# Moved operands of the dense products in the upper half of SBUF, their weights in the lower half

## The chip, the core and the metric

The kernel runs as one program on one core of a Trainium2 chip. The metric is the time of one execution in device microseconds; the figure that counts is the median over several runs. One execution was profiled as well, and its rows are what the text below quotes. Lower is better.

## What is computed

A decoder trunk of two layers over 1024 tokens with a width of 1024, all in float32. Layer 0 has a forgetting attention with a pooling mixer, layer 1 an RWKV-7 time mix; each is followed by a gated feed-forward block of width 2816.

```
def _swiglu(h, w_gate, w_up, w_down):
    return (jax.nn.silu(h @ w_gate) * (h @ w_up)) @ w_down

def reference(x, ...):
    for layer in range(DEPTH):
        h = _rmsnorm(x, mix_norm[layer])
        if layer % 2 == 0:
            y = _fox_pool_mixer(h, hy_w_in[e], ...)      # h @ w_in, attention, pooling, @ w_out
        else:
            y, v_first = _rwkv7_time_mix(h, ...)          # xr @ w_r, xk @ w_k, xv @ w_v, scan, @ w_o
        x = x + y
        x = x + _swiglu(_rmsnorm(x, ffn_norm[layer]), ...)
    return x
```

## The kernel before

**Dense products.** Tokens lie along the free dimension in two halves of 512, features along the partitions. A dense product therefore multiplies a 128x128 block of weights, which TensorE holds still, with a 128x512 tile of inputs, which it moves through. Each float32 operand is split into a high and a low part in float32r, and `mm3` (line 155) forms a product as three matmuls: high by high (line 162), low moved part by high weights (line 163), high moved part by low weights (line 164):

```
nc.tensor.matmul(out, wh, xh, start=(first and i == 0), stop=False)
nc.tensor.matmul(out, wh, xl, start=False, stop=False)
nc.tensor.matmul(out, wl, xh, start=False, stop=(last and i == n - 1))
```

There are 3088 such triples of the full size that the change is about, 9264 matmuls. In the profile a row `mm<-uh,whi` reads: output `mm` (or `fm`), moved tile `uh`, weights `whi`; the letter h or l at the end says high or low part.

**Weights.** `load_part` (line 141) brings a 128x512 piece by DMA into `wraw`, casts it on ScalarE to `whi` and subtracts on VectorE for `wlo`. Weight tiles come from the pool `wf` from the start on, from the pool `w4` for the last stage, and a few small ones from `wl`. `pair` (line 249) makes the two parts of a moved tile, `part` (line 256) fills them.

**Stages.** (1) `fox` (line 313): the normed input H lies in the pool `h`; projections, attention and pooling run woven into each other. (2) Output projection, from the same pool `h`. (3) First feed-forward block, lines 1355 to 1367: half 0 moves tiles from the pool `u`; half 1 moves tiles from the pool `m1` (their name in the profile is `h1`), and most of half 1 is kept as filler `f1`. (4) `rw.dense(0, ...)`: projections of the time mix for half 0; the moved tiles again come from `u`. (5) The time mix of half 0 (`rw.job`), with `f1` woven in. (6) `tail(0, ...)` (line 1381), the output projection and second feed-forward block of half 0, moving tiles `h` and `g` from the pool `tail0`, woven into `rw.dense(1, ...)`, which moves `mx` tiles from the pool `mb`, and then into the time mix of half 1. (7) `tail(1, ...)` from the pool `tail1`, alone at the end.

**What sets the order and the addresses.** The instructions are put in order at build time from the order of the code and from when buffers come free. Pools are stacks: a pool of side left gets the next free bytes from the bottom of each partition, a pool of side right from the top down, and a closed pool gives its bytes back. The side and the order in which pools are opened thus set every address. A tile of a dense product, moved or weights, takes 2048 bytes of each partition, and the blocks of weights within it start every 512 bytes.

The lines that the change touches most are 323 (side of the pool `fox`), 353 and 1280 (which buffers a split goes to), 1267 to 1272 and 1303 to 1304 (opening of pools), 1332 to 1341, 1366, 1390, 1402, 1407, 1419 and 1450.

Of the kernel before, what the change touches and what calls it, by code (L numbers as in the profile page):

```python
# [197 lines left out]
def chain(*gens):  # L198
    for g in gens:
        yield from g  # L200
# [48 lines left out]
def pair(k, pool, tag, bufs, n=HN):  # L249

    hi = pool.tile([P, n], F32R, tag=tag, name=nm(k, tag + "h"), bufs=bufs)
    lo = pool.tile([P, n], F32R, tag=tag, name=nm(k, tag + "l"), bufs=bufs)
    return hi, lo


def part(k, hl, raw):
    hi, lo = hl
    k.nc.scalar.copy(hi, raw)  # L258
    k.nc.vector.tensor_tensor(lo, raw, rd(hi), ALU.subtract)  # L259
    return hi, lo  # L260


def use_ln_exp(k, after=None):

    i = k.nc.scalar.preload_act_table_set("natural_log_exp_and_others")
    if after is not None:
        k.tc.add_manual_dep(i.ins, after.ins.name, mybir.DependencyInfo(mybir.DependencyClass.NoSync, mybir.DependencyReason.DATA),
                            reason="act table")
# [44 lines left out]
def fox(k, ins, H, hpool, xpools, y, then, r_att):  # L313
# [6 lines left out]
    k.tmpbufs=5  # L320
    nc, tc = k.nc, k.tc
    ctx = ExitStack()
    ap_ = ctx.enter_context(tc.tile_pool(name="fox", bufs=1, side="right", reuse_waits="tile"))

    def tmp(n):
        return ap_.tile([P, HN + 16], F32, tag="tmp", name=nm(k, n), bufs=k.tmpbufs)
# [19 lines left out]
    def load_x(half, at={}):  # L346
        n = Norm(k, None, tmp)
        for kt in range(KT):
            if kt in at:
                at[kt]()  # L350
            t = xtile(k, xpools[half])[:, 1:]
            nc.sync.dma_start(t, ins["xT"][kt * P:(kt + 1) * P, half * HN:half * HN + HN])
            hi, lo = H[half][kt] = pair(k, hpool, "h", 32)
            nc.scalar.activation(hi, t, AF.Copy, scale=cvec(k, "mix0", kt))  # L354
            nc.vector.scalar_tensor_tensor(lo, t, cvec(k, "mix0", kt), rd(hi), ALU.mult, ALU.subtract)
            n.add(t)
            xs[half].append(t)
        return n
# [314 lines left out]
def make_h(k, norm, gain, x, acc, out, rs=None):  # L673
    nc = k.nc
    rs = rs or norm.rstd()
    for kt in range(KT):
        t = norm.tile("hn")
        nc.vector.scalar_tensor_tensor(t, x[kt], cvec(k, gain, kt), rs, ALU.mult, ALU.mult)
        out[kt] = part(k, pair(k, *acc), t)


def ffn(k, ins, L, halves, H, X, acc, tp, groups, after=None, silu=True, fb0=0):
    nc = k.nc

    def project(w):
        o = {half: pmm(k) for half in halves}
        for c in range(2):
            for half in halves:
                yield from mm3(k, o[half], [(blk(w, kt), H[half][kt]) for kt in range(4 * c, 4 * c + 4)], c == 0, c == 1)
        return o  # L690

    def down(n, fb0, acts, last):
        per = max(1, 4 // n)
        cur = None
        for half, m in [(half, m) for half in halves for m in range(8)] if last else [(half, m) for m in range(8) for half in halves]:
            if cur != m // per:
                cur = m // per
                w = []
                for f in range(0, n, 4):
                    c = min(4, n - f)  # L700
                    w.append(load_part(k, ins[f"wd{L}"][per * cur:per * cur + per, :, fb0 + f:fb0 + f + c].rearrange("m p f c -> p m f c"), P, per * c * P))
            o = pmm(k)
            yield from mm3(k, o, [(blk(w, (m % per) * n + i), acts[fb0 + i, half]) for i in range(n)])
            nc.vector.tensor_tensor(X[half][m], o, X[half][m], ALU.add)  # L704
            if last:
                after(half, m)


    behind = iter(())
    for gi, n in enumerate(groups):  # L710
        acts, sgs = {}, {}
        for fb in range(fb0, fb0 + n):
            g = yield from project(load_w(k, ins[f"wg{L}"][fb]))
            for half in halves:
                sg = sgs[half] = tp.tile([P, HN], F32, tag="nt", name=nm(k, "sg"), bufs=k.ntbufs)
                if silu:
                    k.last_silu = nc.scalar.activation(sg, g[half], AF.Silu)
                elif silu is None and k.sigm:
                    k.last_sig = nc.scalar.activation(sg, g[half], AF.Sigmoid)
                    nc.vector.tensor_tensor(sg, g[half], sg, ALU.mult)  # L720
                else:
                    nc.scalar.activation(sg, g[half], AF.Exp, scale=-1.0)
                    nc.scalar.activation(sg, sg, AF.Ln, bias=1.0)
                    nc.scalar.activation(sg, sg, AF.Exp, scale=-1.0)
                    nc.vector.tensor_tensor(sg, g[half], sg, ALU.mult)  # L725
            yield from behind
            behind = iter(())
            u = yield from project(load_w(k, ins[f"wu{L}"][fb]))
            for half in halves:
                sg = sgs[half]  # L730
                nc.vector.tensor_tensor(sg, u[half], sg, ALU.mult)
                acts[fb, half] = part(k, pair(k, *acc), sg)
        behind = down(n, fb0, acts, after and gi == len(groups) - 1)
        fb0 += n
    yield from behind
# [497 lines left out]
def build(ctx, tc, ins, outs, dbg=None, stop=99):  # L1233
    nc = tc.nc
    k = K()
# [11 lines left out]
    def pool(n, side="left"):  # L1247
        c = ExitStack()
        p = c.enter_context(tc.tile_pool(name=n, bufs=1, side=side, reuse_waits="tile"))
        return c, p  # L1250
# [13 lines left out]

    stream(k, 1)
    use_ln_exp(k)
    c_x0, x0 = pool("x0")
    c_wf, wf = pool("wf", "right")
    c_x1, x1 = pool("x1", "right")
    xp = (x0, x1)  # L1270
    c_h, hpool = pool("h")
    c_ps, k.ps = psum("ps0")
    k.mm, k.sbufs = (k.ps, "mm", 3), 2
    k.wp, k.wbufs, k.rawbufs, k.ntbufs = wf, 5, 2, 6
# [2 lines left out]
    LATE = 3  # L1277

    def split_y(kt, half):
        sp[kt, half] = part(k, pair(k, hpool, "h", 32), y[kt][half])  # L1280

    def out_tile(half, m):
        XT[half][m] = xtile(k, xp[half])
# [16 lines left out]
                nc.vector.tensor_tensor(x, o, x, ALU.add)  # L1300

    fox(k, ins, H, hpool, xp, y, oproj_early(), [3.2, 2.8, 2.8])
    c_m, mp = pool("m1", "right")
    c_t, tp = pool("t1", "right")
    wo = [load_part(k, ins["w_out"][4 * i:4 * i + 4, :, LATE * P:LATE * P + P].rearrange("m p c -> p m c"), P, 512) for i in range(2)]
    w7 = load_w(k, ins["w_out"][7])
    def out_block(half, m, last):
# [22 lines left out]
            on[1].add(x)  # L1330
    c_h.close()
    c_wl, wl = pool("wl")
    c_u, u = pool("u")
    U, M = (u, "u", 40), (mp, "h1", 24)
    make_h(k, on[0], "ffn0", X[0], U, H[0], rs0)
    c_ps.close()
# [1 line left out]
    c_ps, k.ps = psum("ps1")  # L1338
    k.mm = (k.ps, "mm", 4)

    norms = [Norm(k, tp), Norm(k, mp)]

    cover = [lambda: None, lambda: ahead(project, 0)]

# [18 lines left out]
    run(ffn(k, ins, 0, (0, 1), H, X, U, tp, G0, fb0=sum(GP)))  # L1363
    run(ffn(k, ins, 0, (0,), H, X, U, tp, G1, after0, True, n))
    rw.ln_exp, rw.mx, rw.wl_bufs, k.sigm = False, U, 2, True
    f1 = chain(ffn(k, ins, 0, (1,), H, X, M, mp, GP, silu=None), ffn(k, ins, 0, (1,), H, X, M, mp, G2, after0, None, n))
    f1 = using(k, f1, mm=(pf, "fm", 2), ntbufs=3)
    lead, share = (96, 0)
    ahead(f1, lead)
    weave(rw.dense(0, XT[0], wl, tp), (f1, share))  # L1370
    for c in (c_u, c_wl, c_x0, c_t, c_ps):
        c.close()
    c_ps, k.ps = psum("ps2")
    k.sbufs = 3
# [3 lines left out]
    use_ln_exp(k, k.last_sig)  # L1378
    k.mm, k.sigm, rw.ln_exp = (pf, "fm", 2), False, True

    def tail(half, p, ng, silu):

        norm = Norm(k, p)

        def project():
            sp = []
            for kt in range(KT):
                t = norm.tile("y")
                nc.sync.dma_start(t, rw.dt(f"y{kt}_{half}"))
                sp.append(part(k, pair(k, p, "h", 16), t))  # L1390
            yield 0
            for m in range(8):
                hl = load_w(k, ins["w_o"][m])
                o = pmm(k)
                yield from mm3(k, o, [(blk(hl, kt), sp[kt]) for kt in range(KT)])
                x = X[half][m] = p.tile([P, HN], F32, tag="x4", name=nm(k, "x"), bufs=8)
                nc.sync.dma_start(x, rw.dt(f"x{m}_{half}"))
                nc.vector.tensor_tensor(x, o, x, ALU.add)
                norm.add(x)

        def rest():
            make_h(k, norm, "ffn1", X[half], (p, "h", 16), H[half])

            def after1(half, m):
                nc.sync.dma_start(outT[m * P:(m + 1) * P, toks(half)], X[half][m])

            yield from ffn(k, ins, 1, (half,), H, X, (p, "g", 2 * ng), p, (4, 4, 4, 4, 4, 2), after1, silu)

        return project(), rest()

# [5 lines left out]
    c_ps, k.ps = psum("ps3")  # L1416
    k.mm, k.ntbufs = (k.ps, "mm", 4), 6
    c_t, tp = pool("tail0")
    project, rest = (using(k, g, mm=(pf, "fm", 2), ntbufs=3) for g in tail(0, tp, 4, False))
    Y1 = 1  # L1420
    if Y1:
        next(project)
    run(f1)
    c_m.close()
    c_mb, mb = pool("mb", "right")
    rw.mx, rw.wl_bufs, rw.ln_exp = (mb, "mx", 36), 2, "0"=="1"
    d1 = rw.dense(1, XT[1], mb, mb, ((2, "k", 1), (3, "v", 4), (0, "r", 5)))
# [19 lines left out]
    c_ps.close()  # L1447
    c_ps, k.ps = psum("ps5")
    c_w, wp4 = pool("w4")
    c_l, lp = pool("tail1")  # L1450
    project, rest = (using(k, g, mm=(k.ps, "mm", 3), wp=wp4, wbufs=7, ntbufs=3) for g in tail(1, lp, 8, True))
    weave(project, (fill, TS))
    run(fill)
    run(rest)
    for c in (c_l, c_w, c_t, c_wf, c_ps, c_pf):
        c.close()


# [89 lines left out]
```

## Time and profile before

| | before |
|---|---|
| median of 3 runs | 2720.83 us (2717.3 to 2724.43) |
| the profiled execution | 2725.7 us |
| its span, first to last instruction | 2723.9 us, mean granted clock 0.992 |
| busy time of TensorE's matmuls, 15368 records | 2665.5 us (98%) |
| busy time of its weight loads | 2080.5 us (76%) |
| busy time of VectorE, ScalarE | 1725.1 us (63%), 1297.9 us (48%) |

The profile counts a matmul as busy from its start to the modelled end of its last result, so neighbouring matmuls overlap, and a busy share of 98% says only that TensorE hardly rests. How fast it goes is read from the distance between the starts of two matmuls, or from how many of them fit into a stretch of time. The weight load of the next matmul runs beside the current one and has its own rows (PEld).

### The profile page before, as it was taken

How to read it: one execution, taken by the hardware profiler on the slowest of the kernel's cores; microseconds unless marked ns; L12 is line 12 of the kernel's file. 1: busy time of each engine (PE TensorE's matmuls, PEld its weight loads, DVE VectorE, ACT ScalarE, POOL GpSimd, SP SyncE). 2: the span in 40 equal slices, each digit the busy share in tenths (PEclk: the TensorE clock that was granted, in tenths of full speed). 3: DMA queues.
4: the chain of work that ended last, by engine and by line, in shares of the span. 5: the costliest groups of instructions: out<-in, count | busy, mean ns of one | idle time of the engine just before them, and what ended most of it. 6: DMA issues, size and time to landing. Idle time of an engine off the chain costs nothing.

```text
span 2723.9 us, 40262 instructions
## 1 busy us (share of the span) xinstructions
PE 2665.5 (98%) x15368; PEld 2080.5 (76%) x15368; DVE 1725.1 (63%) x2940; ACT 1297.9 (48%) x2297; POOL 50.0 (2%) x139
## 2 busy tenths in 40 slices
PE   9999999999999999999999999999999999999999
PEld 6777778778888777777777677777777777788887
DVE  7777684653336655975995676569769856544443
ACT  7555564442224766534644467655445344333232
POOL 1000000000001000000000000000000000000000
PEclk9999999999999999999999999999999999999999
DMA  4111131233333445423533534454344236333332
GB/s 134 57 51 57 41 96 51 82 93 94 94 96 112 159 164 179 132 88 95 175 93 98 185 105 154 163 184 128 90 136 136 86 98 201 104 97 97 97 97 93
DMA packets 170241, 306.11 MB, mean 112 GB/s; under 512 B 18608, under 2 KB 25904, under 8 KB 170048
## 3 DMA queue, kind: packets, MB, share of 16 engines
q1 hardware_dynamic: 156224, 278.38, 32.8%
q10 hardware_dynamic: 13824, 25.17, 2.5%
q8 instruction: 120, 1.97, 0.3%
q14 instruction: 73, 0.60, 0.1%
HBM read 257.04 MB, written 46.43 MB: 111 GB/s over the span
## 4 chain that ended last, share of the span: by engine, by line
PE 82%; DVE 11%; ACT 3%; DMA 2%; issue 2%; SPq 0%; ACTq 0%; DVEq 0%
PE mm L162 17%; PE mm L163 16%; PE mm L164 16%; PE fm L162 7%; PE fm L164 6%; PE fm L163 6%; DVE wlo L151 2%; PE mm L174 1%; DVE nu L1109 1%; DVE pd L1107 1%; PE s L1057 1%; PE o L1174 1%; PE s L1162 1%; PE s L1168 1%; PE o L1187 1%
## 5 line engine op out<-in xcount | busy, mean ns | idle before, releaser
L150 ACT CAST whi<-wraw 128x512 fp32r<-128x512 f32 x738 | 453.1, 616 | 891.6 <-PE mm L163 493.0
L151 DVE TENSOR_TENSOR wlo<-wraw,whi 128x512 fp32r<-128x512 f32 x738 | 500.9, 683 | 455.9 <-ACT whi L150 445.5
L162 PE MATMUL mm<-hh,whi 128*128 128x512 f32 x864 | 345.1, 401 | 5.8 <-ACT hh L354 5.7
L164 PE MATMUL mm<-hh,wlo 128*128 128x512 f32 x864 | 340.4, 394 | 0.0
L163 PE MATMUL mm<-hl,whi 128*128 128x512 f32 x864 | 339.5, 394 | 0.0
L164 PE MATMUL mm<-uh,wlo 128*128 128x512 f32 x728 | 287.3, 395 | 1.4 <-DVE wlo L151 1.4
L162 PE MATMUL mm<-uh,whi 128*128 128x512 f32 x728 | 287.7, 397 | 0.9 <-DVE x L1315 0.9
L163 PE MATMUL mm<-ul,whi 128*128 128x512 f32 x728 | 287.5, 396 | 0.0
L162 PE MATMUL fm<-h1h,whi 128*128 128x512 f32 x528 | 220.7, 418 | 14.0 <-DVE sg L725 9.9
L163 PE MATMUL fm<-h1l,whi 128*128 128x512 f32 x528 | 210.1, 398 | 0.1
L164 PE MATMUL fm<-h1h,wlo 128*128 128x512 f32 x528 | 209.7, 397 | 0.5 <-DVE wlo L151 0.5
L162 PEld LDWEIGHTS mm<-hh,whi 128*128 128x128 f32 x864 | 162.8, 189 | 42.6 <-ACT hh L354 6.5
L164 PEld LDWEIGHTS mm<-hh,wlo 128*128 128x128 f32 x864 | 162.8, 188 | 35.9 <-DVE wlo L151 0.6
L163 PEld LDWEIGHTS mm<-hl,whi 128*128 128x128 f32 x864 | 163.2, 189 | 33.6 <-DVE hl L259 1.5
L162 PE MATMUL fm<-hh,whi 128*128 128x512 f32 x416 | 174.5, 420 | 3.2 <-ACT hh L258 2.7
L164 PE MATMUL fm<-hh,wlo 128*128 128x512 f32 x416 | 167.9, 404 | 0.0
L163 PE MATMUL fm<-hl,whi 128*128 128x512 f32 x416 | 167.7, 403 | 0.2 <-DVE hl L259 0.2
L162 PEld LDWEIGHTS mm<-uh,whi 128*128 128x128 f32 x728 | 136.4, 188 | 38.7 <-issue 3.5
L163 PEld LDWEIGHTS mm<-ul,whi 128*128 128x128 f32 x728 | 136.6, 188 | 35.8 <-issue 1.1
L164 PEld LDWEIGHTS mm<-uh,wlo 128*128 128x128 f32 x728 | 136.5, 188 | 35.0 <-DVE wlo L151 2.2
L704 DVE TENSOR_TENSOR x<-mm,x 128x512 f32<-128x512 f32 x96 | 66.2, 692 | 122.8 <-PE mm L164 122.5
L162 PEld LDWEIGHTS fm<-h1h,whi 128*128 128x128 f32 x528 | 100.4, 190 | 48.1 <-DVE sg L725 12.3
(338 smaller groups left out, 4642.5 us busy)
## 6 DMA issues: line engine op xcount, KB each, us to landing
wraw<-in_wg_dram SPq DMA_DIRECT2D x176, 256.0 KB, 2.8
wraw<-in_wu_dram SPq DMA_DIRECT2D x176, 256.0 KB, 2.7
wraw<-in_wd_dram SPq DMA_DIRECT2D x176, 256.0 KB, 2.7
wraw<-in_w_in_dram SPq DMA_DIRECT2D x52, 256.0 KB, 2.9
x<-in_xT_dram SPq DMA_DIRECT2D x32, 256.0 KB, 4.6
x<-x SPq DMA_DIRECT2D x32, 256.0 KB, 3.6
wraw<-in_w_k_dram SPq DMA_DIRECT2D x32, 256.0 KB, 2.8
wraw<-in_w_v_dram SPq DMA_DIRECT2D x32, 256.0 KB, 3.0
```

Of the source, the lines that this page charges most:

```text
L150: k.nc.scalar.copy(hi[0:p, 0:n], raw[0:p, 0:n])
L151: k.nc.vector.tensor_tensor(lo[0:p, 0:n], raw[0:p, 0:n], rd(hi[0:p, 0:n]), ALU.subtract)
L162: nc.tensor.matmul(out, wh, xh, start=(first and i == 0), stop=False)
L163: nc.tensor.matmul(out, wh, xl, start=False, stop=False)
L164: nc.tensor.matmul(out, wl, xh, start=False, stop=(last and i == n - 1))
L174: k.nc.tensor.matmul(out[n * q:n * q + n], w[:, n * j:n * j + n], xs[j], start=c == 0, stop=c + g == len(xs), tile_position=(0, n * q))
L704: nc.vector.tensor_tensor(X[half][m], o, X[half][m], ALU.add)
L1057: nc.tensor.matmul(scs[h][:, 128 * c:128 * c + 128], bk[HS[h], 4 * b + c], ZL[h][HS[h], i, 4 * b + c], start=True, stop=True)
L1107: nc.vector.tensor_tensor(pv, nu[:, j + 1:32, j:j + 1].broadcast_to([P, n, j]), nu[:, j:j + 1, 0:j].broadcast_to([P, n, j]), ALU.mult)
L1109: nc.vector.tensor_tensor(nu[:, j + 1:32, 0:j], nu[:, j + 1:32, 0:j], pv, ALU.add)
L1162: nc.tensor.matmul(z[HS[h], i], ZL[h][:, i, c, 0:64], SV[h][:, i, c], start=True, stop=True)
L1168: nc.tensor.matmul(u[HS[h], i], XR[HS[h], i, c, 0:64], zs[HS[h], i], start=True, stop=True)
```

## The change

The pools of weights go to the left side, the pools of moved tiles to the right side. The pool `h` goes: H and the split attention outputs get the pool `m1` for twelve of sixteen pairs and a new pool `h2` for the other four. `m1` is opened at the start and stays open to the end; `tail(0, ...)` takes its pairs from it too, instead of from `tail0`, so that its inputs, its activations and those of the block before it share one ring of 24 buffers. A small new pool `n1` takes the norm's and the gate's work tiles of half 1. Operations, shapes and counts of instructions stay.

The core of the diff:

```
-    ap_ = ctx.enter_context(tc.tile_pool(name="fox", bufs=1, side="right", reuse_waits="tile"))
+    ap_ = ctx.enter_context(tc.tile_pool(name="fox", bufs=1, side="left", reuse_waits="tile"))
...
-            hi, lo = H[half][kt] = pair(k, hpool, "h", 32)
+            hi, lo = H[half][kt] = pair(k, *hpool[8 * half + kt >= 12])
...
+    c_wf, wf = pool("wf")
     c_x0, x0 = pool("x0")
-    c_wf, wf = pool("wf", "right")
+    c_m, mp = pool("m1", "right")
     c_x1, x1 = pool("x1", "right")
+    c_h, h2 = pool("h2", "right")
-    c_h, hpool = pool("h")
+    hpool = (mp, "h1", 24), (h2, "h2", 8)
...
-    c_m, mp = pool("m1", "right")
-    c_t, tp = pool("t1", "right")
+    c_t, tp = pool("t1")
...
-    c_u, u = pool("u")
+    c_n, np_ = pool("n1", "right")
+    c_u, u = pool("u", "right")
...
-    f1 = chain(ffn(k, ins, 0, (1,), H, X, M, mp, GP, silu=None), ...)
+    f1 = chain(ffn(k, ins, 0, (1,), H, X, M, np_, GP, silu=None), ...)
...
-                sp.append(part(k, pair(k, p, "h", 16), t))
+                sp.append(part(k, pair(k, *hs), t))
...
-    project, rest = (... for g in tail(0, tp, 4, False))
+    project, rest = (... for g in tail(0, tp, 4, False, M, M))
...
-    c_l, lp = pool("tail1")
+    c_l, lp = pool("tail1", "right")
```

Where the built programs put the pools (bytes from the start of a partition; the middle of the 224 KiB is 114688):

| pool, what for | first to last byte before | first to last byte after |
|---|---|---|
| `wf`, weights | 204768 to 229344 | 4608 to 29184 |
| `w4`, weights of the last stage | 76288 to 109056 | 51712 to 84480 |
| `wl`, small weights of the time mix | 21248 to 31488 | 64256 to 74496 |
| `h` (after: `m1` and `h2`), moved | 21248 to 86784 | 180192 to 229344 and 147168 to 163552 |
| `u`, moved | 31488 to 113408 | 75488 to 157408 |
| `m1`, moved | 132832 to 188128 | 180192 to 229344 |
| `mb`, moved | 85728 to 188128 | 61152 to 163552 |
| `tail0` (after: `m1`), moved | 4608 to 76288 | 180192 to 229344 |
| `tail1`, moved | 109056 to 197120 | 92128 to 180192 |
| `fox`, attention | 87488 to 188128 | 45824 to 146464 |
| `core`, `core2`, time mix | 4608 to 132736, 76288 to 204416 | 29184 to 157312, 51712 to 179840 |

Of the 9264 full-size matmuls, those that move a tile of `u` are 2184, of `h` 1344, of `tail0` 1776, of `m1` 1584, of `mb` 600, of `tail1` 1776; the weights are in `wf` for all but the last, which has `w4`.

The order of instructions changes in few places, all of them where a split waits for a buffer. On ScalarE, at the splits of the eight `y` tiles of `tail(0, ...)` (the cast at line 258, out `hh` from `y`; `whi` are casts of weights, `sg` gates of `f1`), before:

```order
L150 CAST whi_14433<-wraw_14435 128x512
L258 CAST hh_14258<-y_14256 128x512
L258 CAST hh_14264<-y_14262 128x512
L258 CAST hh_14270<-y_14268 128x512
L150 CAST whi_14439<-wraw_14441 128x512
L258 CAST hh_14276<-y_14274 128x512
L150 CAST whi_14475<-wraw_14477 128x512
L258 CAST hh_14282<-y_14280 128x512
L258 CAST hh_14288<-y_14286 128x512
```

The same place after the change, where the tiles are named `h1h` since they are cut from `m1`:

```order
L150 CAST whi_14583<-wraw_14585 128x512
L722 ACTIVATE sg_14473<-fm_14448 128x512
L258 CAST h1h_14285<-y_14283 128x512
L723 ACTIVATE sg_14473<-sg_14473 128x512
L258 CAST h1h_14291<-y_14289 128x512
L724 ACTIVATE sg_14473<-sg_14473 128x512
L258 CAST h1h_14297<-y_14295 128x512
L150 CAST whi_14615<-wraw_14617 128x512
L258 CAST h1h_14303<-y_14301 128x512
```

The first four splits stay near their place, the last four move behind four to five casts of weights and into the last gate of `f1`: their buffers come free only as TensorE ends the last products of `f1`. The second place is ScalarE in the attention of the last pair of heads, at the splits of the attention outputs for the output projection (`x` here is such an output). Before:

```order
L150 CAST whi_3898<-wraw_3900 128x512
L120 CAST ph_3551<-pt_3549 128x512
L258 CAST hh_3710<-x_2740 128x512
L150 CAST whi_4027<-wraw_4029 128x512
L480 CAST KA_102<-ak_2932 64x512
L542 ACTIVATE pt_3587<-s_3584,ncumT 128x512
```

And after:

```order
L150 CAST whi_3901<-wraw_3903 128x512
L120 CAST ph_3554<-pt_3552 128x512
L258 CAST h1h_3713<-x_2743 128x512
L258 CAST h2h_3725<-x_1460 128x512
L258 CAST h2h_3733<-x_1686 128x512
L150 CAST whi_4030<-wraw_4032 128x512
```

Splits into `h2` come earlier than their turn in the old ring. TensorE's own order differs only by some matmuls that change places with neighbours.

More of the change, by code (lines that the diff above doesn't have):

```diff
@@ L1279, in split_y @@
     def split_y(kt, half):
-        sp[kt, half] = part(k, pair(k, hpool, "h", 32), y[kt][half])
+        sp[kt, half] = part(k, pair(k, *hpool[8 * half + kt >= 12]), y[kt][half])
     def out_tile(half, m):
@@ L1339, in build @@
     k.mm = (k.ps, "mm", 4)
-    norms = [Norm(k, tp), Norm(k, mp)]
+    norms = [Norm(k, tp), Norm(k, np_)]
     cover = [lambda: None, lambda: ahead(project, 0)]
@@ L1365, in build @@
     rw.ln_exp, rw.mx, rw.wl_bufs, k.sigm = False, U, 2, True
-    f1 = chain(ffn(k, ins, 0, (1,), H, X, M, mp, GP, silu=None), ffn(k, ins, 0, (1,), H, X, M, mp, G2, after0, None, n))
+    f1 = chain(ffn(k, ins, 0, (1,), H, X, M, np_, GP, silu=None), ffn(k, ins, 0, (1,), H, X, M, np_, G2, after0, None, n))
     f1 = using(k, f1, mm=(pf, "fm", 2), ntbufs=3)
@@ L1370, in build @@
     weave(rw.dense(0, XT[0], wl, tp), (f1, share))
-    for c in (c_u, c_wl, c_x0, c_t, c_ps):
+    for c in (c_u, c_wl, c_t, c_x0, c_ps):
         c.close()
@@ L1379, in build, with tail @@
     k.mm, k.sigm, rw.ln_exp = (pf, "fm", 2), False, True
-    def tail(half, p, ng, silu):
+    def tail(half, p, ng, silu, hs, gs):
         norm = Norm(k, p)
@@ L1401, in rest @@
         def rest():
-            make_h(k, norm, "ffn1", X[half], (p, "h", 16), H[half])
+            make_h(k, norm, "ffn1", X[half], hs, H[half])
             def after1(half, m):
                 nc.sync.dma_start(outT[m * P:(m + 1) * P, toks(half)], X[half][m])
-            yield from ffn(k, ins, 1, (half,), H, X, (p, "g", 2 * ng), p, (4, 4, 4, 4, 4, 2), after1, silu)
+            yield from ffn(k, ins, 1, (half,), H, X, gs, p, (4, 4, 4, 4, 4, 2), after1, silu)
         return project(), rest()
@@ L1418, in build @@
     c_t, tp = pool("tail0")
-    project, rest = (using(k, g, mm=(pf, "fm", 2), ntbufs=3) for g in tail(0, tp, 4, False))
+    project, rest = (using(k, g, mm=(pf, "fm", 2), ntbufs=3) for g in tail(0, tp, 4, False, M, M))
     Y1 = 1
@@ L1423, in build @@
     run(f1)
-    c_m.close()
+    c_n.close()
     c_mb, mb = pool("mb", "right")
@@ L1449, in build @@
     c_w, wp4 = pool("w4")
-    c_l, lp = pool("tail1")
-    project, rest = (using(k, g, mm=(k.ps, "mm", 3), wp=wp4, wbufs=7, ntbufs=3) for g in tail(1, lp, 8, True))
+    c_l, lp = pool("tail1", "right")
+    project, rest = (using(k, g, mm=(k.ps, "mm", 3), wp=wp4, wbufs=7, ntbufs=3) for g in tail(1, lp, 8, True, (lp, "h", 16), (lp, "g", 16)))
     weave(project, (fill, TS))
@@ L1454, in build @@
     run(rest)
-    for c in (c_l, c_w, c_t, c_wf, c_ps, c_pf):
+    for c in (c_l, c_m, c_w, c_t, c_wf, c_ps, c_pf):
         c.close()
```

## The prediction

> **What bounds the kernel now.** I read the page first, for the share of each engine and the chain that ended last:
>
> ```profile
> span 2723.9 us, 40262 instructions
> PE 2665.5 (98%) x15368; PEld 2080.5 (76%) x15368; DVE 1725.1 (63%) x2940; ACT 1297.9 (48%) x2297; POOL 50.0 (2%) x139
> PE 82%; DVE 11%; ACT 3%; DMA 2%; issue 2%; SPq 0%; ACTq 0%; DVEq 0%
> ```
>
> TensorE rests for 58 us in all, and 82% of the chain is its matmuls. A change that alters no operation can thus move the time by the rate at which matmuls follow each other, or by a new wait. The rate is read next, from how much fits into two stretches in which TensorE does almost nothing but full-size products, and from three stretches to which the sum comes back (columns: stretch, its length, busy time and count of TensorE, then the other engines):
>
> ```profile
> core 0: us, PE busy (x) PEld busy (x) DVE busy (x) ACT busy (x) POOL busy (x), PEclk, DMA share, GB/s
> 500.00:860.00 360.00, 360.00 (x1542) 288.68 (x1541) 159.76 (x244) 122.53 (x200) 0.00 (x0) 1.00 0.31 95
> 1090.00:1540.00 450.00, 433.03 (x3700) 329.31 (x3699) 342.71 (x593) 206.96 (x389) 8.99 (x30) 0.98 0.37 117
> 1570.00:1790.00 220.00, 215.96 (x906) 164.66 (x907) 132.37 (x202) 140.95 (x234) 0.15 (x2) 0.98 0.45 144
> 1790.00:2240.00 450.00, 436.26 (x3767) 331.50 (x3765) 345.36 (x599) 220.12 (x415) 10.59 (x35) 0.98 0.39 121
> 2410.00:2700.00 290.00, 290.00 (x1281) 240.20 (x1280) 119.83 (x181) 85.17 (x141) 0.00 (x0) 1.00 0.32 97
> ```
>
> In the first feed-forward block a matmul takes 360 / 1542 = 233.5 ns, in the second block of half 1 it takes 290 / 1281 = 226.4 ns. Both run at the full granted clock (1.00), in both TensorE never rests, and the operation is the same. So there are two rates already, 7.1 ns apart, and what divides them is what this change may touch. Starts in the timeline give the same pair; the first and the last of eleven consecutive starts in each of the two stretches, and of fifteen in the projections of the time mix of half 1:
>
> ```profile
> 699.74 0.40 PE L163 MATMUL mm<-ul,whi 128*128 128x512 f32 x1
> ...
> 702.07 0.40 PE L164 MATMUL mm<-uh,wlo 128*128 128x512 f32 x1
> ```
>
> ```profile
> 2499.99 0.39 PE L162 MATMUL mm<-hh,whi 128*128 128x512 f32 x1
> ...
> 2502.26 0.39 PE L163 MATMUL mm<-hl,whi 128*128 128x512 f32 x1
> ```
>
> ```profile
> 1679.17 0.39 PE L162 MATMUL mm<-mxh,whi 128*128 128x512 f32 x1
> ...
> 1682.34 0.39 PE L164 MATMUL mm<-mxh,wlo 128*128 128x512 f32 x1
> ```
>
> That is 2.33 / 10 = 233 ns, 2.27 / 10 = 227 ns and 3.17 / 14 = 226 ns. At 233 ns `u` is moved against `wf`, at 226 to 227 ns `tail1` against `w4` and `mb` against `wf`. Last, all products of line 162 by their moved tile and weights (shortest/median/longest in ns); a matmul of the slow rate ends at 396, one of the fast rate at 389 or 390:
>
> ```profile
> L162 PE MATMUL mm<-uh,whi x728: 387/396/796, 496.1 to 1057.2; 128*128 128x512 f32 x182
> L162 PE MATMUL fm<-h1h,whi x528: 387/390/797, 866.9 to 1567.6; 128*128 128x512 f32 x176
> L162 PE MATMUL fm<-hh,whi x416: 389/396/802, 1571.6 to 2347.4; 128*128 128x512 f32 x139
> L162 PE MATMUL mm<-mxh,whi x200: 388/389/628, 1583.8 to 1790.4; 128*128 128x512 f32 x100
> L162 PE MATMUL fm<-gh,whi x176: 388/396/794, 1867.7 to 2359.7; 128*128 128x512 f32 x176
> L162 PE MATMUL mm<-gh,whi x176: 387/389/500, 2409.5 to 2719.2; 128*128 128x512 f32 x176
> L162 PE MATMUL mm<-uh,wlhi x8: 389/390/400, 1024.2 to 1059.1; 128*128 128x512 f32 x8
> L164 PE MATMUL mm<-uh,wllo x8: 392/396/397, 1025.4 to 1059.6; 128*128 128x512 f32 x8
> ```
>
> **What divides the two rates.** At first sight it is the half of SBUF: `tail1` (moved) lies mostly high and `w4` low and is fast; `u` and `tail0` lie low under high weights and are slow. Two places of these rows speak against it. The fifteen `mx` matmuls from 1679.17 move tiles between bytes 93920 and 110304 in the built program, in the lower half, against `wf` high up, and run at 226 ns; `u` reaches over the same bytes, against the same weights, at 233. And the last two rows move tiles of `u` too, low, against `wl`, also low: 390 on line 162, but 396 on line 164, after which TensorE turns back to weights in `wf`. So the rate belongs to a pair, the tile being moved and the weights loaded meanwhile for the next matmul.
>
> The addresses of the built program name such a pair. I divide each pool's first byte by 64; blocks of weights start every 512 bytes and tiles every 2048, so the remainder holds for all of a pool's tiles. Before: `wf` 32, `w4` 0, `wl` 0; moved: `h` 0, `u` 0, `tail0` 0, `m1` 32, `mb` 32, `tail1` 0. Equal remainders: `m1` and `mb` on `wf`, `tail1` on `w4`, `u` on `wl`; these are just the rows at 226 to 227 ns, or 389 to 390. Unequal: `h`, `u`, `tail0` on `wf`; these are just the rows at 233 ns, or 396. No row is left over. After: `wf` 0, `w4` 0, `wl` 0, and every moved pool, `m1`, `h2`, `u`, `mb` and `tail1`, 32. Not one pair is equal any more. The reason is plain from the stacks: the top one begins at 229344, remainder 32, the bottom one at 4608, remainder 0, and all weights now grow from one and all moved tiles from the other.
>
> What the rows do not show is the sign: before, the unequal pairs have weights at 32 and moved tiles at 0, afterwards it is the other way about. I take a shift by 32 to cost the same in both directions, since modulo 64 it is the same shift.
>
> **The sum.** 5304 of the 9264 matmuls (`u` 2184, `h` 1344, `tail0` 1776) are slow now and stay slow: nothing. The other 3960 go from fast to slow, at 6.0 ns each by the starts and 7.1 by the stretches; I take 6.6, between them.
>
> - `tail1`, 1776 matmuls, alone on TensorE: 1776 x 6.6 = 11.7 us.
> - `mb`, 600 matmuls: 4.0 us. TensorE rests 220 - 216 = 4 us in that stretch, so if rests shrank instead, 2 us at least.
> - `m1`, 1584 matmuls, of which 864 + 432 = 1296 are woven into the time mix:
>
> ```profile
> 1090.00:1540.00 450.00, 298.57 (x864) 163.76 (x863) 11.66 (x17) 10.52 (x17) 0.98 0.37 117
> 1090.00:1540.00 450.00, 171.21 (x432) 82.49 (x432) 11.66 (x17) 0.98 0.37 117
> ```
>
> The rows are those of the high tiles (lines 162 and 164) and of the low tiles (line 163). The 288 outside cost 288 x 6.6 = 1.9 us. The 1296 inside would cost 8.6 us, but TensorE rests 17 us of these 450 for steps of the time mix on VectorE, and a longer product before such a step shortens the rest behind it. Ends 0 and 8.6; I take two thirds, 5.7, since TensorE is busy for 96% of the stretch and most products follow another product.
> - Neighbours in the attention: in the built order 173 times an attention product follows a dense one (now 0 against 32, afterwards 32 against 32) and 57 times a dense one follows a full-width attention product (equal now, unequal afterwards). (57 - 173) x 6.6 ns = -0.8 us.
> - Moved splits: the `y` splits of `tail(0, ...)` wait for buffers that `f1` gives back.
>
> ```profile
> L258 ACT CAST hh<-y x16: 607/621/622, 1534.5 to 2273.3; 128x512 fp32r<-128x512 f32 x16
> ```
>
> The first of them starts at 1534.5 and TensorE wants them at 1571.6 (row `fm<-hh,whi`). The last buffers come free when half 1's inputs are read for the last time; after that stand the down products of two tiles, 2 x 3 x 8 = 48 matmuls or about 11 us, and four splits of 0.62 us fit. Nothing, and at most 3 us if that cover fails. Queued behind them on ScalarE are weight casts, of which several are ready ahead. The earlier splits into `h2` wait for nothing new: nothing, and below nothing has no reason, as TensorE starts those products when the attention's last outputs are there.
>
> Sum: 11.7 + 4.0 + 1.9 + 5.7 - 0.8 = 22.5 us. The profiled execution took 2725.7 us, 1.8 over its span and 4.9 over the median; it would become 2748.2, and the median 2720.8 + 22.5 = 2743.3 us. Lower end of this case: (1776 + 288) x 6.0 ns + 2 - 1 = 13.4, so 2734; upper end: 3960 x 7.1 ns = 28.1 and 3 for the splits, and the 3.5 us by which runs lie off their median, so 2756.
>
> **Where the Trainium skill says otherwise.** The rows above show that which weights are loaded beside a moved tile changes its rate: `uh` at 390 with `wl` next, at 396 with `wf` next. The Trainium skill, "TensorE: Matmul & The Clock Gate", section "Part 2: What happens when you issue a matmul", says that TensorE has two independent read ports and that loading the next weights takes no read bandwidth from the running matmul; "SBUF — State Buffer", section "Who interferes with whom", says "PE and ACT never wait on anyone." By that rule no placement matters and the sum is 0; the trace does not agree, by these 6 ns.
>
> **Rivals.** (a) Faster: the rate is set by the halves, or only weights at 32 under moved tiles at 0 are slow, and not the reverse. Then all 5304 slow matmuls become fast: 5304 x 6.6 = 35.0 us less, 2686 us; with a third lost where `h` and half of `tail0` are woven into other work about 28 us less, 2693. For it: the cleanest fast stretch is high over low, and no row of before shows moved tiles at 32 over weights at 0. Against it: the low `mx` matmuls and the row of `uh,wlhi`, for halves; for the one-sided rule there is only symmetry. It decides from the first feed-forward block on.
> (b) No change: the rate is not the placement's doing, or placement does not reach the end: 2720.8. Against it: the same line 162 with the same moved pool has two medians. For it: nothing but that causes were read from groups that differ in more than one thing.
> (c) Slower by a wait: the shared ring of 24 buffers makes splits late in `tail(0, ...)` as well, where activations, inputs and outputs of the product now draw on one ring. Each new wait of a split pair is about 1.3 us with cast and subtraction; TensorE has filler in the time mix. It adds up to 3 us to my case and makes none of its own.
>
> **How the numbers follow.** My case, slower by the sum, 0.80; (a) 0.14, most of it for the one-sided rule; (b) 0.06. A measurement of this kernel tells about 0.3% (8.2 us) from no change; the lower end of my case, 13.4 us, lies beyond that, so slower 0.80, faster 0.14, same 0.06. The range reaches from 2726 to 2756 us: it leaves out (a), most of (b), and little above.
>
> **What would show it.** Right: the stretch of the last block, 226.4 ns a matmul now, goes to about 233, as do the rows `mx` and `h1`; medians of `mm<-gh,whi` and `mm<-mxh,whi` go from 389 to 395 or 396; the first feed-forward block stays at 233.5. Wrong: the first block goes to 226 (then rival a), or the last block stays at 226. If the rates come as said but the time doesn't, TensorE's rest between 1090 and 1540 must have shrunk by more than a third of 8.6 us.

## The result, and the profile after

The changed kernel takes 2740.2 us (median of 4 runs, 2736.1 to 2745.8) beside 2722.6 us of the kernel before (4 runs, 2717.3 to 2725.4): a ratio of 1.0064, 95% interval 1.0048 to 1.0080, or 13.1 to 21.8 us more. The profiled execution took 2738.6 us. The head of its page, with span, busy time by engine and the chain that ended last:

```profile
span 2736.8 us, 40265 instructions
PE 2677.9 (98%) x15368; PEld 2077.4 (76%) x15368; DVE 1725.3 (63%) x2940; ACT 1297.6 (47%) x2297; POOL 50.2 (2%) x139
PE 79%; DVE 14%; ACT 2%; issue 2%; DMA 2%; SPq 0%; DVEq 0%; ACTq 0%
```

The span grew by 12.9 us and TensorE's busy time by 12.4; the other engines did the same work in the same time. The same five stretches as before (stretch, length, then busy time and count of TensorE, its weight loads, VectorE, ScalarE and GpSimd, granted clock, DMA share, GB/s):

```profile
500.00:860.00 360.00, 360.00 (x1542) 289.23 (x1541) 159.59 (x243) 122.77 (x200) 0.00 (x0) 1.00 0.32 95
1090.00:1540.00 450.00, 435.50 (x3702) 328.02 (x3702) 343.41 (x595) 208.57 (x390) 8.99 (x30) 0.99 0.38 119
1570.00:1790.00 220.00, 216.35 (x893) 162.31 (x894) 131.75 (x201) 139.62 (x232) 0.15 (x2) 0.98 0.43 139
1790.00:2240.00 450.00, 434.93 (x3773) 331.85 (x3772) 346.46 (x600) 220.29 (x415) 11.35 (x35) 0.99 0.39 123
2410.00:2700.00 290.00, 290.00 (x1245) 233.57 (x1244) 114.90 (x175) 82.99 (x137) 0.00 (x0) 1.00 0.32 95
```

In the last block a matmul now takes 290 / 1245 = 232.9 ns (226.4 before), in the first block 360 / 1542 = 233.5 ns as before, and 893 instead of 906 matmuls fit into the stretch of `mb`. But the stretch in which the time mix and `f1` are woven holds 3702 matmuls, where it held 3700. Then the products of line 162, and one group of line 164, by moved tile and weights (shortest/median/longest in ns, first and last start in us):

```profile
L162 PE MATMUL mm<-uh,whi x728: 388/396/793, 496.3 to 1057.0; 128*128 128x512 f32 x182
L162 PE MATMUL fm<-h1h,whi x1120: 387/396/1322, 867.0 to 2362.3; 128*128 128x512 f32 x187
L162 PE MATMUL mm<-mxh,whi x200: 392/396/628, 1583.9 to 1793.3; 128*128 128x512 f32 x100
L162 PE MATMUL mm<-gh,whi x176: 394/396/502, 2413.4 to 2732.1; 128*128 128x512 f32 x176
L162 PE MATMUL mm<-uh,wlhi x8: 394/395/396, 1023.9 to 1058.9; 128*128 128x512 f32 x8
L164 PE MATMUL mm<-uh,wllo x8: 392/395/396, 1025.0 to 1059.3; 128*128 128x512 f32 x8
```

Every group shown stands at 395 or 396; before, `f1`, `mx`, `g` of half 1 and `uh,wlhi` stood at 389 or 390. In the timeline, the first and the last of eleven consecutive starts of the last block, 2.33 / 10 = 233 ns apart:

```profile
2499.72 0.40 PE L163 MATMUL mm<-gl,whi 128*128 128x512 f32 x1
...
2502.05 0.40 PE L164 MATMUL mm<-gh,wlo 128*128 128x512 f32 x1
```

First and last starts of line 162 give the time stage by stage. Up to the last `uh`: 1057.2 before, 1057.0 after, -0.2 us. From there to the first `mxh`, the time mix of half 0 with `f1`: 526.6 and 526.9, +0.3. From the first `mxh` to the last: 206.6 and 209.4, +2.8. From there to the last product of `tail(0, ...)` (2359.7 and 2362.3): 569.3 and 569.0, -0.3. From there to the end: 359.5 and 369.8, +10.3. These are the 12.9 us. They are one execution of each kernel; the +0.3 above all is no clean measure, as the section on the prediction shows.

### The profile page after: what moved, and what is told of

It is laid out like the page before. It is cut to its first block, busy times and chain, and to the rows that moved or that the text cites. A ratio compares the mean times of both kernels' runs of the same rounds, so it can differ in the third digit from the quotient of the medians.

```text
span 2736.8 us, 40265 instructions
## 1 busy us (share of the span) xinstructions
PE 2677.9 (98%) x15368; PEld 2077.4 (76%) x15368; DVE 1725.3 (63%) x2940; ACT 1297.6 (47%) x2297; POOL 50.2 (2%) x139
## 4 chain that ended last, share of the span: by engine, by line
PE 79%; DVE 14%; ACT 2%; issue 2%; DMA 2%; SPq 0%; DVEq 0%; ACTq 0%
PE mm L162 17%; PE mm L163 16%; PE mm L164 16%; PE fm L162 7%; PE fm L163 6%; PE fm L164 6%; DVE wlo L151 2%; DVE ZL L1065 1%; PE mm L174 1%; DVE nu L1109 1%; DVE pd L1107 1%; PE s L1162 1%; PE o L1174 1%; PE o L1187 1%; PE s L1168 1%
## 5 line engine op out<-in xcount | busy, mean ns | idle before, releaser
L162 PE MATMUL fm<-h1h,whi 128*128 128x512 f32 x1120 | 469.5, 420 | 20.4 <-DVE sg L725 11.0
L164 PE MATMUL fm<-h1h,wlo 128*128 128x512 f32 x1120 | 448.0, 400 | 0.5 <-DVE wlo L151 0.5
L163 PE MATMUL fm<-h1l,whi 128*128 128x512 f32 x1120 | 447.9, 400 | 0.0
L164 PEld LDWEIGHTS fm<-h1h,wlo 128*128 128x128 f32 x1120 | 212.2, 189 | 54.1 <-issue 2.2
L163 PEld LDWEIGHTS fm<-h1l,whi 128*128 128x128 f32 x1120 | 212.6, 190 | 49.7 <-issue 5.3
L164 PE MATMUL mm<-hh,wlo 128*128 128x512 f32 x416 | 164.4, 396 | 0.0
L163 PE MATMUL mm<-hl,whi 128*128 128x512 f32 x416 | 164.3, 396 | 0.0
L162 PE MATMUL mm<-hh,whi 128*128 128x512 f32 x416 | 164.2, 396 | 0.0
L162 PE MATMUL mm<-h1h,whi 128*128 128x512 f32 x336 | 138.2, 413 | 6.0 <-ACT h1h L354 6.0
L164 PE MATMUL mm<-h1h,wlo 128*128 128x512 f32 x336 | 134.4, 400 | 0.0
L162 PEld LDWEIGHTS mm<-hh,whi 128*128 128x128 f32 x416 | 78.1, 188 | 19.6 <-ACT whi L150 0.5
```

## The experiments

Addresses are those of the built programs. "Distance" means the first byte of the moved pool less that of the weights' pool, modulo 256. Before, it is 32 for `h`, `u` and `tail0`, and 0 for `m1`, `mb`, `tail1` on `w4` and `u` on `wl`. After, it is 224 for every pair. Most kernels shift a stack by a spacer, one small tile that nothing reads:

```
+    def spacer(n, side="left"):
+        c, p = pool("spacer", side)
+        nc.gpsimd.memset(p.tile([P, n // 4], F32, ...), 0.0)
+        return c
```

Each matmul spacing below is a count in a stretch in which TensorE never rests, unless something else is said.

**The rule of the prediction, on the changed kernel.** Two kernels make remainders modulo 64 equal: for all pairs, by lifting the whole bottom stack, or for the last stage alone, by lifting `w4`. First:

```
     ...
+    c_sp = spacer(32)
     c_wf, wf = pool("wf")
```

> The changed kernel with 32 bytes put below its bottom stack of pools, so that weights and moved tiles both have remainder 32 on division by 64; halves, ring and order stay those of the changed kernel. Remainder theory: every full-size dense stretch runs at 226 to 227 ns a matmul; sure gains over the changed kernel's 2740.2 us are tail1 11.7, u 14.4 and mb 4.0, the 4704 woven matmuls of h, m1 and the former tail0 give between 9 and 31 more: 2680 to 2701 us, likeliest 2692. Theory of halves, and theory that the loss is a wait in the shared ring: nothing changes, 2740 us, dense stretches stay at 233 ns.

Measured: 2743.9 us (4 runs, before 2723.6), ratio 1.0077, 1.0062 to 1.0093. First and last block:

```profile
500.00:860.00 360.00, 360.00 (x1542) 289.31 (x1542) 159.71 (x244) 122.34 (x199) 0.00 (x0) 1.00 0.32 95
2410.00:2700.00 290.00, 290.00 (x1244) 233.67 (x1243) 115.41 (x174) 83.71 (x138) 0.00 (x0) 1.00 0.32 95
```

Equal remainders modulo 64, and still 233.5 and 233.1 ns. My rule falls here. The second kernel:

```
     ...
+    c_sp = spacer(32)
     c_w, wp4 = pool("w4")
```

> The changed kernel with 32 bytes put below the pool w4 alone, so that only the last stage's pairs are equal again. Remainder theory: the last stage goes from 233 to 226 ns a matmul, 1776 x 6.6 = 11.7 us less than 2740.2, about 2728.5 us, all else as in the changed kernel. Theory of halves or of a wait: 2740 us.

Measured: 2742.8 us, ratio 1.0073, 1.0059 to 1.0086; the last block:

```profile
2410.00:2700.00 290.00, 290.00 (x1244) 232.43 (x1243) 114.61 (x173) 84.03 (x139) 0.00 (x0) 1.00 0.32 95
```

The same miss for one stage by itself: at a distance of 192 bytes 290 / 1244 = 233.1 ns.

**The rule on the kernel before, halves kept.** The spacer of 32 bytes goes under the kernel before's bottom stack, ahead of `x0`; weights stay high, `u` low.

> The kernel before with the same 32 bytes below its bottom stack: h, u, tail0, tail1 and w4 get remainder 32, as wf, m1 and mb have; moved tiles of h, u, tail0 stay in the lower half, wf in the upper. Remainder theory: the stretch 500 to 860 us goes from 233.5 to 226.5 ns a matmul; 2184 x 6.6 = 14.4 us for u are sure, h and tail0 add between 6 and 20: 2688 to 2702 us against 2722.6. Theory of halves: no pair changes its half, 2722 us and 233.5 ns.

Measured: 2710.3 us, ratio 0.9952, 0.9938 to 0.9966. The first block:

```profile
500.00:860.00 360.00, 360.00 (x1571) 294.54 (x1571) 166.03 (x254) 125.83 (x205) 0.00 (x0) 1.00 0.33 101
```

229.2 ns, neither of the two rates. So halves aren't the cause, for the halves are those of before; but a distance of 64 isn't as good as 0 either, as the rule modulo 64 has it. Left is the distance over a longer period. That 0 and 256 modulo 512 both run at 226 to 227 ns in the kernel before (`tail1` on `w4`; `mb` on `wf`) makes the period 256 or a divisor of it.

**One woven term by itself.** In the kernel before, `m1` is put 32 bytes lower, at a distance of 224; of the other pools only `t1`, which lies below it and holds work tiles, moves along.

```
     ...
+    c_sp = spacer(32, "right")
     c_m, mp = pool("m1", "right")
```

> The kernel before with 32 bytes put above the pool m1 alone (top stack), so that only f1's 1584 products, mostly woven into the time mix, become unequal (moved 0, weights 32). By the prediction's terms: 1.9 + 5.7 = 7.6 us more, about 2730. By what the changed kernel's trace shows (3702 matmuls in the stretch 1090 to 1540 against 3700): the woven ones are absorbed, 0 to 2 us more, about 2724. In both cases f1's products follow each other at 233 ns instead of 227 to 229.

Measured: 2725.8 us (11 runs; before 2723.6, 15 runs), ratio 1.0006, 0.9997 to 1.0014: -0.8 to 3.8 us, where the terms of the prediction for `m1` (5.7 and 1.9) give 7.6. The rate of its products did change, while the other large groups kept theirs (`fm<-h1h` 390 before, `mxh` 389 before):

```profile
L162 PE MATMUL fm<-h1h,whi x528: 390/396/800, 867.3 to 1570.3; 128*128 128x512 f32 x176
L162 PE MATMUL mm<-mxh,whi x200: 389/389/628, 1585.0 to 1791.6; 128*128 128x512 f32 x100
```

TensorE's longest waits between 1090 and 1540, in the list of waits (engine, line, what it waited for: us in total, times, longest); of the kernel before, of the changed one, and of this one:

```profile
PE fm L162 <- DVE sg L725: 9.9, 5, 4.0
```

```profile
PE fm L162 <- DVE sg L725: 7.6, 4, 3.5
```

```profile
PE fm L162 <- DVE sg L725: 8.1, 4, 3.6
```

The gate of `f1` on VectorE (line 725) ends when it ends. TensorE reaches it later with longer products and waits less, by about 2 us in these profiles.

**Distance 0 everywhere, with the old halves and with the new.** A constant `k.nb`, which no instruction of the built program reads, loses half of its columns; the bottom stack begins 32 bytes lower. Nothing else changes, and no spacer is added. The same edit goes into both kernels:

```
-    k.nb = k.const.tile([P, 16], F32, tag="nb", name="nb")
+    k.nb = k.const.tile([P, 8], F32, tag="nb", name="nb")
```

> The changed kernel with its bottom stack 32 bytes lower (half of a small constant that nothing reads is dropped), so that moved address minus weights address is a multiple of 256 in every full-size pair; halves, ring and order are those of the changed kernel. Theory of the distance modulo 256: all dense stretches at 226.8 ns; sure gains over 2740.2 us are u 14.2, tail1 11.5, mb 3.9; woven products add 0 to 15: 2696 to 2711 us, likeliest 2703. Theory that only what lay equal before (top stack on top stack, bottom on bottom) is quick, whatever the distance: stays at 233 ns and 2740 us.

Measured, in the changed kernel: 2707.4 us (5 runs, before 2723.5), ratio 0.9943, 0.9930 to 0.9955. First and last block:

```profile
500.00:860.00 360.00, 360.00 (x1586) 297.13 (x1585) 169.53 (x260) 128.42 (x209) 0.00 (x0) 1.00 0.34 101
2410.00:2700.00 290.00, 290.00 (x1280) 239.75 (x1280) 117.77 (x178) 81.99 (x135) 0.00 (x0) 1.00 0.32 95
```

> The kernel before with its bottom stack 32 bytes lower in the same way, so that every full-size distance is a multiple of 256; its halves stay (u, h and tail0 low, wf high). Theory of the distance modulo 256: u's stretch at 226.8 ns, 14.2 us sure, h and tail0 between 6 and 20 more: 2690 to 2703 us, about as the changed kernel so aligned. Theory of halves beside the distance: this one stays at least 8 us behind the changed kernel so aligned. Theory that the changed kernel's ring costs waits: this one is some us ahead of it.

Measured, in the kernel before: 2703.9 us (5 runs), ratio 0.9925, 0.9911 to 0.9939, the best of all kernels here. First block, and four groups of line 162:

```profile
500.00:860.00 360.00, 360.00 (x1585) 296.76 (x1584) 167.46 (x257) 127.55 (x208) 0.00 (x0) 1.00 0.34 103
```

```profile
L162 PE MATMUL mm<-uh,whi x728: 387/389/793, 493.9 to 1041.0; 128*128 128x512 f32 x182
L162 PE MATMUL mm<-mxh,whi x200: 389/389/500, 1567.5 to 1772.9; 128*128 128x512 f32 x100
L162 PE MATMUL fm<-gh,whi x176: 387/389/793, 1848.7 to 2338.9; 128*128 128x512 f32 x176
L162 PE MATMUL mm<-gh,whi x176: 388/389/497, 2388.8 to 2698.4; 128*128 128x512 f32 x176
```

Both run at 227 ns in the first block. The placement in halves gives nothing: with it the kernel takes 3.4 us more than without, by the medians of 5 runs each, whose ranges overlap (2706.2 to 2710.6 and 2700.0 to 2707.3 us). Of the 19.6 us by the medians (20.8 by these rows against those of before) the first block and the projections, where `u` is moved alone, bring 561.1 - 547.1 = 14.0, which is 2184 x 6.4 ns. The pool `h`, woven into the attention, brings 2.2 (the first `uh` starts at 493.9, before at 496.1), where 1344 x 6.6 ns would be 8.9. `tail0` brings 569.3 - 566.0 = 3.3 where it is woven into the second time mix, and up to 206.6 - 205.4 = 1.2 in the stretch of `mb`, in which its first products run; 1776 x 6.6 ns would be 11.7.

**The steps between.** Three more kernels set other distances for `u`: 160 and 128 by spacers of 64 and 96 bytes in the changed kernel, 96 by one of 64 in the kernel before.

> The changed kernel with 64 bytes below its bottom stack: every full-size distance is 160 modulo 256. Distance seen so far: 0 gives 226.8 ns, 32, 192 and 224 give 233.3, 64 gives 229 to 230. Theory of a short window of quick distances from 0 upwards: 233 ns, 2740 us. Theory that distances half-way round are quick as well: under 230 ns, about 2710 us.

> The changed kernel with 96 bytes below its bottom stack: every full-size distance is 128 modulo 256. Theory of a short window of quick distances: 233 ns, 2740 us. Theory of a period of 128: 226.8 ns and about 2703 us. Theory of a slope from 0 over 64: between 229 and 233 ns.

> The kernel before with the lower stack 64 bytes higher: first block, h1 and tail0 pairs come to a distance of 96 bytes mod 256, the halves m1, mb and tail1/w4 stay at 0. Theory of the short window (only 0 and 64 are quick): first block at 233 ns, time as the kernel before, 2720 to 2728 us. Rival (the cost climbs with the distance, 0 at 226.8, 64 at 229, 128 at 233): first block at 230 to 232, time 2711 to 2719 us.

Measured, one run each: 2747.7, 2737.9 and 2719.4 us (before 2723.5 in the first two, 2723.2 beside the last). The first lies 7.7 us above what was expected by the short window and the last 0.6 below; with one run each, the rate in the first block decides and not the time. Their first blocks, one fence for each kernel in that order:

```profile
500.00:860.00 360.00, 360.00 (x1536) 288.72 (x1535) 158.22 (x242) 121.51 (x198) 0.00 (x0) 1.00 0.32 94
```

```profile
500.00:860.00 360.00, 360.00 (x1543) 289.27 (x1542) 159.84 (x244) 122.60 (x200) 0.00 (x0) 1.00 0.32 95
```

```profile
500.00:860.00 360.00, 360.00 (x1542) 288.90 (x1541) 159.66 (x244) 122.14 (x198) 0.00 (x0) 1.00 0.32 95
```

With the runs above the first block has been timed at every distance in steps of 32 bytes. 360 us divided by the count gives:

| distance of `u` from `wf`, bytes | 0 | 32 | 64 | 96 | 128 | 160 | 192 | 224 |
|---|---|---|---|---|---|---|---|---|
| ns a matmul | 227.1 | 233.5 | 229.2 | 233.5 | 233.3 | 234.4 | 233.5 | 233.5 |

The distances 32, 64 and 96 were measured with the old halves, 128 to 224 with the new ones, 0 with both. Only 0 and, less so, 64 are quick. As 128 is not, the period is 256 and no divisor of it. That the cost climbs with the distance is refuted by the value at 32, and again by that at 96, which is above that at 64.

## Why the prediction was right, and where it was not

**The bound and the pair.** Right for long stretches. TensorE's matmul rate is what moved, and it follows the addresses of the moved tile and the weights. In the distance-0 kernel made from the one before, moving one stack by 32 bytes takes 19.6 us away, with the same operations on the same halves of SBUF. The Trainium skill, "TensorE: Matmul & The Clock Gate", section "Part 2: What happens when you issue a matmul", says that TensorE has two independent read ports and that loading the next weights takes no read bandwidth from the running matmul; if it is that load which slows the matmul, 227.1 and 233.5 ns for the same stretch do not agree with it.

That it is the load of the next weights, and not the matmul's own, is less sure: in the long stretches both lie in one pool. For it speaks `uh,wllo` of before, at 396 with its own weights at distance 0 and the next at 32. But the eight products of `u` against `wl`, from which the prediction read the pair, do not keep to the rule. They stay at distance 0 where the lower stack of the kernel before is lifted by 32 or 64 bytes, and still go from 390 to 396 and 398 (one fence for each of the two kernels):

```profile
L162 PE MATMUL mm<-uh,wlhi x8: 389/396/423, 1012.3 to 1046.9; 128*128 128x512 f32 x8
```

```profile
L162 PE MATMUL mm<-uh,wlhi x8: 395/398/401, 1024.7 to 1059.7; 128*128 128x512 f32 x8
```

They stand in small groups between products of `u` against `wf` at other distances. So a few products among others do not show what their own pair costs, and the measured rule holds for long runs of one pair only; why the small groups differ stays open.

**The rule.** Wrong in its form. "Equal remainders" modulo 64 was read from pairs whose distances were only 0 and 32, and the change adds only 224. On these three the rule modulo 64 and the measured one, distance 0 modulo 256, say the same, which is why the forecast held; that the change touched no fourth distance is luck. Where the two differ, the rule fails: at 128 (233.3 ns) and 192 (233.5) outright, at 64 (229.2) in part. The step on the sign ("since modulo 64 it is the same shift") fell with it: 32 and 224 happen to cost the same, 64 and 192 don't.

**The sum, stretch by stretch** (predicted terms regrouped by where they fall; measured from the two profiles):

| stretch | predicted, us | measured, us |
|---|---|---|
| to the last `uh`: 96 matmuls of `m1`, neighbours in the attention | 0.6 - 0.8 = -0.2 | -0.2 |
| `f1` with the time mix: 1296 woven, 192 beside it | 5.7 + 1.3 = 7.0 | 0.3 |
| `mb` | 4.0 | 2.8 |
| `tail(0, ...)`, some 190 matmuls of `tail1` in it, splits | 1.2 | -0.3 |
| the last stage, 3 x 529 = 1587 matmuls of `tail1` | 10.5 | 10.3 |
| sum | 22.5 | 12.9 |

The last stage came out to the point, 1587 x 6.5 ns; its count is that of line 162 in the kernel before, from the last product of `tail(0, ...)` to the end, times three (columns: TensorE's busy time and count, then its weight loads):

```profile
2359.70:2720.00 360.30, 205.31 (x529) 99.03 (x528) 1.00 0.31 96
```

The counts of `m1` by stretch (96, 1296, 192) come from the timeline.

The first mis-sized term is the woven one, "I take two thirds, 5.7". With `m1` alone moved, all of `m1` cost 2.2 us by the medians (-0.8 to 3.8) where the prediction has 5.7 and 1.9. The +0.3 of the table is not that price, for four things meet in this stage:

- Between two products of `f1` the ordinary distance of starts (up to 300 ns) went from 229.0 to 233.3 ns. It had not been 226 before, so the step is 4.3 ns and not 6.6: 5.9 us over 1381 distances.
- The waits for the gate (line 725) went from 9.9 to 7.6 us, as shown above. My own sign for this case, that TensorE's rest between 1090 and 1540 shrinks by more than a third of 8.6 us, was nearly met: 17.0 us before, 14.5 after.
- A new wait came, for a split of `f1` on ScalarE. It is the second mis-sized term, "Nothing, and at most 3 us", and is taken up under rival (c): 2.2 us.
- The granted clock differed. In both profiles it stands at half for 3.4 us at a time, seven times in this stage before and four times after, so about 11.9 and 6.8 us of full clock are lost. That is an estimate of 5.1 us in favour of the profile after, and the kernel with `w4` lifted, below, shows that it isn't a gain of the change.

The first row is a piece of such low clock in the kernel before (0.50, third number from the end). Then this stage in the kernel before, in the changed kernel, and in the one with `w4` lifted, which up to its last stage has the changed kernel's instructions at the same addresses. One fence for each kernel:

```profile
1187.00:1196.00 9.00, 8.00 (x78) 6.22 (x79) 6.32 (x9) 3.05 (x5) 0.00 (x0) 0.50 0.32 91
1057.20:1583.80 526.60, 503.92 (x4035) 384.46 (x4035) 398.05 (x681) 252.50 (x469) 10.47 (x34) 0.98 0.41 128
```

```profile
1057.00:1583.90 526.90, 505.05 (x4036) 381.65 (x4035) 398.11 (x681) 252.34 (x469) 11.36 (x37) 0.99 0.41 128
```

```profile
1056.80:1590.60 533.80, 509.70 (x4035) 385.01 (x4034) 398.27 (x681) 252.44 (x469) 11.37 (x37) 0.98 0.41 126
```

With seven drops of the clock, as before, the same stage of the same instructions takes 533.8 us, 7.2 more than before; its wait for the split is 3.9 us. One execution thus cannot price this stage. With `m1` alone moved, the distances between the same products of `f1` hold 352.2 us beside 349.5 before, and the stage grew by 1.4.

The medians differ by 17.6 us, the profiles by 12.9, just under the interval of 13.1 to 21.8. The profiled execution of before had a mean granted clock of 0.992 and lies 3.1 us above the median of its 4 runs; that of after had 0.995 and lies 1.6 below. An estimate from the runs comes out near the medians: 2.8 for `mb` and 10.3 for the last stage from the profiles, 2.2 for `m1` from its own kernel, 2.2 for the new wait and -0.5 in the two other stretches, 17.0 in all. The forecast of 2743.3 lies 3.1 us above the result, but the sum of 22.5 lies just over the interval. The woven term and `mb` were too large, the split too small, and these errors partly cancel.

**The rivals.** (a) Faster through the halves, or through a one-sided rule: no; the first block stayed at 233.5 with the new halves and goes to 227 with either arrangement at distance 0. Its price of 35.0 us for all 5304 matmuls, 28 with a third lost in woven work, was also too high: the old halves at distance 0 gave 19.6. (b) No change: no. (c) A wait in the shared ring: it exists, but not in the stretch of `tail(0, ...)`, which did not grow (569.3 and 569.0). The prediction asked whether the `y` splits come in time for their own products. It did not ask what they hold up in ScalarE's order, and put the term at nothing. Before, ScalarE splits the last but one activation of `f1` ahead of the last gate (line 722):

```profile
1547.87 0.61 ACT L258 CAST h1h<-sg 128x512 fp32r<-128x512 f32 x1
1549.67 0.60 ACT L722 ACTIVATE sg<-fm 128x512 f32<-128x512 f32 x1
```

In the changed kernel this split comes behind that gate and four `y` splits, and TensorE waits for it:

```profile
1548.66 0.59 ACT L722 ACTIVATE sg<-fm 128x512 f32<-128x512 f32 x1
1554.28 0.61 ACT L258 CAST h1h<-sg 128x512 fp32r<-128x512 f32 x1
1554.95 1.22 PE L162 MATMUL fm<-h1h,whi 128*128 128x512 f32 x2 [2.68 <-ACT h1h L258]
```

In the list of waits between 1057 and 1584, before and after:

```profile
PE fm L162 <- ACT h1h L258: 0.5, 1, 0.5
```

```profile
PE fm L162 <- ACT h1h L258: 2.7, 1, 2.7
```

This wait is 0.2 to 0.5 us in all five kernels with the old pools and 2.5 to 3.9 in all six with the shared ring. At distance 0 it is 3.9 against 0.5, which is 3.4 us more and as much as the two kernels differ by. That the wait is the whole of this difference isn't shown, since the ring was not tried apart from the halves.

## What to carry to other kernels

When identical matmuls run at two rates, read the built addresses of the moved tile and of the weights loaded for the next matmul, and shift one pool by a few bytes before rearranging anything: 32 bytes were worth 0.75% here, while moving whole pools to the other half and missing the distance cost 0.64%. A rule fitted to two values of an address cannot tell its period; scan the steps before building on it. Price a longer operation in full only where its engine has nothing to wait for; in work woven with another engine's steps, here about a quarter to two fifths of the price reached the end (2.2 of 8.9 us for `h`, 3.3 to 4.5 of 11.7 for `tail0`, 2.2 of 7.6 for `m1`). Where splits of two stages share a ring and an engine, ask also what the earlier ones hold up. And price a stage in which the granted clock drops now and then from several executions, not from one profile.

## What the runs showed of the chip

In long stretches, the spacing of float32r matmuls of 128x512 depends on the distance of their moved tile from the weights modulo 256 bytes: 227.1 ns at 0, 229.2 at 64, 233.3 to 234.4 at every other step of 32, all at a granted clock of 1.00 in those stretches. What inside the chip repeats every 256 bytes, whether other types and shapes do the same, and whether there are narrower steps than 32 bytes, no run here shows. In the woven stages the granted clock falls to half for 3.4 us at a time, seven or four times in the same instructions at the same addresses, and the stage took 533.8 or 526.9 us.
